# RWKV's threads: where five results are produced and used in the steps of the recurrence

## The chip, the cores and the metric

One core of one Trainium2 chip runs the program. The metric is device microseconds of one execution, the median of the runs shown.

## The reference

One layer of a bidirectional encoder over 256 positions of width 2048: a projection feeds three mixers (a gated MLP, a Hyena long convolution, RWKV-7), whose outputs are gated and merged, followed by a SwiGLU. The change lies in the RWKV mixer, whose recurrence is

```python
def step(s, inp):
    r_t, w_t, k_t, v_t, a_t, b_t = inp
    sa = jnp.einsum('dbhij,dbhj->dbhi', s, a_t)
    s = s * w_t[..., None, :] + sa[..., :, None] * b_t[..., None, :] + v_t[..., :, None] * k_t[..., None, :]
    return s, jnp.einsum('dbhij,dbhj->dbhi', s, r_t)

_, y = lax.scan(step, s0, (r, w, k, v, a, b))
```

It runs in both directions over 16 heads of 64 channels, and is followed by a norm per head, a bonus term `sum(r * k * r_k) * v` and a gate.

## The kernel before

All dense products are split into float32r parts: a weight piece of 4 k-tiles (128x512) is loaded by a DMA from SP, cast to `wh` on ScalarE (ACT, L222), and the rest `wl` is taken on VectorE (DVE) or GpSimd (POOL, L226). `dense` (L239 to L241) then issues three matmuls 128x256 per k-tile, and yields after each k-tile. The program of GpSimd, VectorE and ScalarE besides holds the recurrence's own work.

The recurrence is in chunks of 64 positions and treats two heads at a time; such a pair is called head 0 to 7 here (`j` in the code). It is written as five generators, each of which walks through all eight heads: `wkv_prep` (decays, keys, bonus), `wkv_scores` (score matmuls L667, their masked evictions L676, transposes of `bk`), `wkv_inverse` (a triangular inverse: 15 steps of two small VectorE operations, L733 and L736, called the substitution here, a round trip of the blocks through DRAM, L742 and L747, a VectorE transpose of what came back, L750, then matmuls L755 and L763), `wkv_chain` (L802, L813, then the four chunk steps: matmuls L855, L861, L874 with the VectorE results `T` L857, `UV` L865 and `sb` L879 between them) and `wkv_norm`. `threads` runs them in rounds: in each round every generator advances by one `yield 1`, and about four k-tiles (`ROUND = 4.0`, 12 matmuls) of the queued dense work are issued among them, so that TensorE has something to do while the other engines work.

```python
                with self.tc.issue_after(self.last.ins):
                    step = next(g, self)
```

So what a generator issues in a step can't stand ahead of the last dense matmul before that step on TensorE. It can stand behind it: each engine runs its instructions in a fixed order, but a scheduler makes that order when the program is built, from its own costs, and lets later instructions pass one whose inputs it takes to be late. The order of an engine is therefore read from the built program, not from the code. Dense work that the recurrence doesn't use up is issued behind it (`drain`).

PSUM tiles: `ps_dn` for the dense work, `ps_big` with two buffers for most of the rest, `ps_inv` and `ps_ch` for inverse and chain.

Of the kernel before, what the change touches and what calls it, by code (L numbers as in the profile page):

```python
# [12 lines left out]
AF = mybir.ActivationFunctionType  # L13
# [3 lines left out]
P = 128  # L17
T = 256
# [172 lines left out]
class Build:  # L191
# [359 lines left out]
    def wkv_prep(self, R, j, front, res):  # L551

        nc = self.nc
        rp = R["rp"]
        V, S, G = nc.vector, nc.scalar, nc.gpsimd
        tl = lambda sh, name, bufs=1: rp.tile([P] + sh, F32, tag=name, name=name, bufs=bufs)
        mult, add = ALU.mult, ALU.add
        rk2, v = front
        r, k = rk2[:, 0, :], rk2[:, 1, :]
# [9 lines left out]
        for i in range(2):  # L569
            for d in range(2):  # L570
                rows = slice(64 * d, 64 * d + 64)
                nc.tensor.matmul(pd[d][:, i * T:(i + 1) * T], wa[rows, i, :],
                                 R["lo"][rows, 1 + i, :], start=True, stop=True, tile_position=(64 * d, 0))
        for d in range(2):
            ps = pd[d]
            tw = tl([T], "tw")
            for i, z in enumerate((tw, ta[:, d, :])):
                c = 16 * i + 8 * d + j
                S.activation(z, ps[:, i * T:(i + 1) * T], AF.Tanh, bias=R["hb"][:, c:c + 1], scale=0.5)
            V.tensor_scalar(tw, tw, 0.5, 0.5, mult, add)  # L580
            if d == 0:
                V.tensor_tensor_scan(cum[:, 0, :], sm[:, :T], tw, 0.0, mult, add)
            else:
                V.tensor_tensor_scan(cum[:, 1, ::-1], sm[:, T:0:-1], tw[:, ::-1], 0.0, mult, add)
            yield 1

        sq = tl([T], "sq")
        S.activation(sq, k, AF.Square, scale=self.vec("k_k", j))
        ps = self.pst("big")
        nc.tensor.matmul(ps[:, :T], self.cst("bones"), sq, start=True, stop=True)  # L590
        yield 1
# [45 lines left out]
        rk = tl([T], "rk")  # L637
        G.tensor_tensor(rk, kd[:, 0, :], kd[:, 1, :], add)
        V.scalar_tensor_tensor(rk, r, self.vec("r_k", j), rk, mult, mult)
        ps = self.pst("big")  # L640
        nc.tensor.matmul(ps[:, :T], self.cst("bones"), rk, start=True, stop=True)
        bon = tl([T], "bon", 2)
# [67 lines left out]
    def wkv_inverse(self, R, j, st):  # L710


        nc = self.nc
        rp = R["rp"]
        V, S, D = nc.vector, nc.scalar, nc.sync
        tl = lambda sh, name, bufs=1: rp.tile([P] + sh, F32, tag=name, name=name, bufs=bufs)
        mult, add = ALU.mult, ALU.add
        d1, Mo = st[1:3]
        Z = tl([2, 2, P], "Z")
        N = Z[:, 1].rearrange("p a (b c) -> p (a b) c", c=16)  # L720
        yield 1
        src = d1.rearrange("d u (q s) e -> (d u q) s e", s=32)
        for i in range(4):
            b = 16 * (i % 2)
            D.dma_start(N[32 * i:32 * i + 32], src[:, b:b + 16, b:b + 16])
        Y, Yt = tl([8, 16], "Y"), Z[:, 0, 0, :40]
        D.dma_start(Y, self.t["rows"])
        yield 1
        yield 1
        for k in range(15):  # L730
            n, w = 15 - k, k // 2 + 1
            z = Yt[:, :w * n].rearrange("p (c t) -> p c t", t=n)
            first = V.tensor_tensor(z, N[:, k, k + 1:].unsqueeze(1).broadcast_to([P, w, n]), Y[:, :w, k:k + 1].broadcast_to([P, w, n]), mult)  # L733
            if k == 0:
                self.tc.keep_in_program_order(first)
            V.tensor_tensor(Y[:, :w, k + 1:], Y[:, :w, k + 1:], z, add)  # L736
            if k % 4 == 3:
                yield 1
        d2 = R["d2"][j % 2]
        for i in range(4):  # L740
            r, b = i // 2, i % 2
            D.dma_start(d2[:, b, :, r, 16 * b:16 * b + 16], Y[32 * i:32 * i + 32])  # L742
        yield 1
        yield from self.after("whole", j - 1)

        XX = tl([4, P], "XX")
        D.dma_start(Z[:, 0].rearrange("p d (u e) -> p (d u) e", e=32), d2.rearrange("(u q) b c r e -> (q b c r) u e", q=4))  # L747
        yield 1
        yield 1
        self.tc.keep_in_program_order(V.transpose(Z[:, 1].rearrange("p a b -> p (a b)"), Z[:, 0].rearrange("p a b -> p (a b)")))  # L750
        blocks = [(d, u, q) for d in range(2) for u in range(4) for q in range(4)]
        ps = self.pst("inv")
        for d, u, q in blocks:
            r, o = slice(32 * q, 32 * q + 32), slice(32 * u, 32 * u + 32)
            nc.tensor.matmul(ps[r, P * d + 32 * u:P * d + 32 * u + 32], Mo[r, d, o], Z[r, 1, d, o], start=True, stop=True,  # L755
                             tile_position=(32 * q, 32 * q))
        T0 = tl([2, P], "T0")
        S.copy(T0, ps[:, :2 * P].rearrange("p (d n) -> p d n", d=2))
        yield 1
        ps = self.pst("inv")  # L760
        for d, u, q in blocks:
            r, o = slice(32 * q, 32 * q + 32), slice(32 * u, 32 * u + 32)
            nc.tensor.matmul(ps[r, P * d + 32 * u:P * d + 32 * u + 32], T0[r, d, o], Z[r, 0, d, o], start=True, stop=True,  # L763
                             tile_position=(32 * q, 32 * q))
        V.tensor_tensor(XX[:, :2], Z[:, 0], ps[:, :2 * P].rearrange("p (d n) -> p d n", d=2), add)
        V.transpose(XX[:, 2:].rearrange("p a b -> p (a b)"), XX[:, :2].rearrange("p a b -> p (a b)"))
        st += XX,
        yield 1
        self.passed.add(("inverse", j))

    def wkv_chain(self, R, j, pre, st):

        nc = self.nc
        rp = R["rp"]
        V, S, G = nc.vector, nc.scalar, nc.gpsimd
        tl = lambda sh, name, bufs=1: rp.tile([P] + sh, F32, tag=name, name=name, bufs=bufs)
        mult, add = ALU.mult, ALU.add
        ident = self.cst("ident")
        v, wcs, bk, ar = pre[:4]
# [2 lines left out]
        at = lambda z, c, h: XX[:, z, 32 * (2 * h + c // 2):32 * (2 * h + c // 2) + 32]  # L782
        X, XT = lambda d, c, h: at(2 - d, c, h), lambda d, c, h: at(3 * d, c, h)
        XF = R["xf"]

        def place(q, d, b):

# [8 lines left out]
        ps = self.pst("inv")  # L796
        for (d, c, h) in units:
            hb = 1 - c % 2
            src, dst = (0, 1) if d == 0 else (1, 0)
# [7 lines left out]
        ps = self.pst("inv")  # L807
        for (d, c, h) in units:
            hb = 1 - c % 2
            src, dst = (0, 1) if d == 0 else (1, 0)  # L810
# [7 lines left out]
                (S.copy if d else V.tensor_copy)(place(q, d, 1 - d), u4(ps[32 * q:32 * q + 32, :P]))  # L818
        yield 1
        self.passed.add(("whole", j))  # L820

        UV = tl([2, 2, 2, P], "UV")
        ps = self.pst("big")
        for i in range(2):
            nc.tensor.transpose(ps[:, i * P:(i + 1) * P], v[:, i * P:(i + 1) * P], ident)
        for par in range(2):
            rows = slice(64 * par, 64 * par + 64)
            src = ps[rows, :T].rearrange("p (c n) -> p c n", n=P).unsqueeze(1).broadcast_to([64, 2, 2, P])
            (S.copy if par else V.tensor_copy)(UV[rows, :, :, par, :], src)

        self.passed.add(("v", j))

        at_step = lambda i: [(d, i if d == 0 else 3 - i) for d in range(2)]


# [14 lines left out]
        for i in range(NC_):  # L850
# [11 lines left out]
            for d, c in at_step(i):  # L862
                hb = 1 - c % 2
                rows = slice(64 * hb, 64 * hb + 64)
# [21 lines left out]
        ps = self.pst("big")  # L886
# [15 lines left out]
    def wkv_norm(self, R, j, pre, ych, ycl):  # L902
# [8 lines left out]
        nc.tensor.matmul(ps[:, :T], self.cst("bones"), yy, start=True, stop=True)  # L911
        V.tensor_tensor(yy, yy, ps[:, :T], ALU.subtract)
        sq2 = tl([T], "sq2")
        yield 1
        S.activation(sq2, yy, AF.Square)
        ps = self.pst("big")
        nc.tensor.matmul(ps[:, :T], self.cst("bones"), sq2, start=True, stop=True)
        pg = self.pst("big")
# [555 lines left out]
```

## Time and profile before

| | |
|---|---|
| runs | 2003.42, 2006.95, 2007.06 us; median 2006.95 us |
| profiled execution | 2000.44 us, its span 1998.7 us |
| busy in the span | TensorE 1892.7, VectorE 1387.7, ScalarE 1068.5, GpSimd 546.5 us |
| recurrence | about 440 to 1030 us of the span |

In the rows below, PE is TensorE's matmuls and PEld its weight loads; in windows, the first number is the length in us, and behind the engines come PEclk, DMA share and GB/s; a bracket at a row's end gives the engine's idle time just before it and what ended that. PEclk is the granted TensorE clock as a share of full speed.

### The profile page before, as it was taken

The numbers are of one execution on the slowest core, as the hardware profiler recorded it, in microseconds if no ns is written. First come the engines' busy times: TensorE is split into PE (matmuls) and PEld (weight loads), VectorE is DVE, ScalarE is ACT, GpSimd is POOL, SyncE is SP. The second block draws the span as 40 slices with busy tenths as digits, with TensorE's granted clock in tenths as the row PEclk, the third lists the DMA queues.
The fourth block names the chain that finished last, engine by engine and source line by source line (L and its number), as shares of the span: only waits on it lengthen the run. The fifth ranks groups of instructions, "written<-read, shape, count | busy, mean of one in ns | idle before, by whom it ended". The sixth has DMA issues, their size and how long they took to land.

```text
span 1998.7 us, 37486 instructions
## 1 busy us (share of the span) xinstructions
PE 1892.7 (95%) x13476; PEld 1679.0 (84%) x13476; DVE 1387.7 (69%) x2556; ACT 1068.5 (53%) x2142; POOL 546.5 (27%) x573
## 2 busy tenths in 40 slices
PE   8999999999879898989999999999999999999997
PEld 6788888879868787888898888888888888888886
DVE  7978798786775767566567777766666666655555
ACT  7665566555444454544445555555555555545443
POOL 3322322235645455545421121111111111100001
PEclk9999999999999899998999999999999999999999
DMA  8454454445433333333355565555555555666664
GB/s 262 158 169 153 135 157 152 138 140 186 123 103 111 90 104 88 115 97 95 97 164 190 190 229 188 188 190 190 191 190 190 190 191 190 189 185 186 188 185 136
DMA packets 215828, 320.39 MB, mean 160 GB/s; under 512 B 62198, under 2 KB 65784, under 8 KB 215640
## 3 DMA queue, kind: packets, MB, share of 16 engines
q1 hardware_dynamic: 209264, 306.13, 49.5%
q0 software_dynamic: 2032, 6.18, 1.0%
q10 hardware_dynamic: 4344, 5.67, 0.9%
q8 instruction: 106, 1.74, 0.4%
q14 instruction: 82, 0.67, 0.1%
HBM read 313.96 MB, written 3.93 MB: 159 GB/s over the span
## 4 chain that ended last, share of the span: by engine, by line
PE 49%; DMA 1%; DVE 1%; ACT 0%; issue 0%; DVEq 0%; POOL 0%; ACTq 0%; POOLq 0%
PE ps_dn L259 23%; PE ps_dn L260 12%; PE ps_big L259 8%; PE ps_big L260 4%; DMA w<-in_wo_dram 0%; PE ps_dn L239 0%; PE ps_dn L240 0%; PE ps_dn L241 0%; PE ps_dn L257 0%; PE ps_dn L256 0%; DVE x L1454 0%; DMA x<-in_xT_dram 0%; DVE wl L226 0%; DVEq L1469 0%; PE ps_ch L855 0%
## 5 line engine op out<-in xcount | busy, mean ns | idle before, releaser
L222 ACT CAST wh<-w 128x512 fp32r<-128x512 f32 x1148 | 704.6, 619 | 570.6 <-PE ps_dn L259 258.0
L226 DVE TENSOR_TENSOR wl<-w,wh 128x512 fp32r<-128x512 f32 x945 | 718.2, 768 | 380.6 <-ACT wh L222 371.8
L226 POOL TENSOR_TENSOR wl<-w,wh 128x512 fp32r<-128x512 f32 x203 | 271.1, 1340 | 378.7 <-ACT wh L222 335.7
L259 PE MATMUL ps_dn<-gw,wh 128*128 128x512 f32 x704 | 246.3, 392 | 0.0
L259 PE MATMUL ps_big<-gw,wh 128*128 128x512 f32 x704 | 246.0, 391 | 0.0
L270 PE MATMUL ps_dn<-hw,wh 128*128 128x512 f32 x640 | 232.1, 402 | 11.9 <-DVE x L400 7.0
L259 PE MATMUL ps_dn<-hid,wh 128*128 128x512 f32 x660 | 233.2, 396 | 0.0
L239 PE MATMUL ps_dn<-hw,wh 128*128 128x256 f32 x688 | 213.6, 311 | 0.0
L241 PE MATMUL ps_dn<-hw,wl 128*128 128x256 f32 x688 | 199.5, 290 | 3.3 <-DVE wl L226 2.6
L260 PE MATMUL ps_dn<-hid,wl 128*128 128x256 f32 x704 | 198.7, 282 | 0.0
L240 PE MATMUL ps_dn<-hw,wh 128*128 128x256 f32 x688 | 198.5, 289 | 0.0
L260 PE MATMUL ps_dn<-gw,wl 128*128 128x256 f32 x704 | 197.6, 281 | 0.0
L260 PE MATMUL ps_big<-gw,wl 128*128 128x256 f32 x704 | 197.4, 280 | 0.0
L271 PE MATMUL ps_dn<-hw,wl 128*128 128x256 f32 x640 | 180.0, 281 | 0.0
L259 PEld LDWEIGHTS ps_big<-gw,wh 128*128 128x128 f32 x704 | 131.8, 187 | 28.7
L259 PEld LDWEIGHTS ps_dn<-gw,wh 128*128 128x128 f32 x704 | 131.8, 187 | 28.6
L270 PEld LDWEIGHTS ps_dn<-hw,wh 128*128 128x128 f32 x640 | 121.2, 189 | 39.6 <-ACT th L1344 5.6
L259 PEld LDWEIGHTS ps_dn<-hid,wh 128*128 128x128 f32 x660 | 124.1, 188 | 30.0
L239 PEld LDWEIGHTS ps_dn<-hw,wh 128*128 128x128 f32 x688 | 134.4, 195 | 6.7 <-issue 3.1
L241 PEld LDWEIGHTS ps_dn<-hw,wl 128*128 128x128 f32 x688 | 134.4, 195 | 4.7 <-DVE wl L226 3.0
L240 PEld LDWEIGHTS ps_dn<-hw,wh 128*128 128x128 f32 x688 | 134.6, 196 | 1.1
L260 PEld LDWEIGHTS ps_dn<-gw,wl 128*128 128x128 f32 x704 | 133.4, 190 | 0.1
(404 smaller groups left out, 3714.9 us busy)
## 6 DMA issues: line engine op xcount, KB each, us to landing
w<-in_wgu_dram SPq DMA_DIRECT2D x352, 256.0 KB, 3.0
w<-in_wgt_dram SPq DMA_DIRECT2D x192, 256.0 KB, 3.0
w<-in_wdn_dram SPq DMA_DIRECT2D x176, 256.0 KB, 2.9
w<-in_wc_dram SPq DMA_DIRECT2D x108, 256.0 KB, 3.0
w<-in_wb_dram SPq DMA_DIRECT2D x96, 256.0 KB, 3.0
w<-in_wbr_dram SPq DMA_DIRECT2D x96, 256.0 KB, 2.7
w<-in_wo_dram SPq DMA_DIRECT2D x64, 256.0 KB, 3.1
w<-in_wav_dram SPq DMA_DIRECT2D x32, 256.0 KB, 3.6
```

Of the source, the lines that this page charges most:

```text
L222: nc.scalar.copy(wh[:, :m], w[:, :m])
L226: e.tensor_tensor(wl[:, :m], w[:, :m], wh[:, :m].bitcast(F32), ALU.subtract)
L239: mm(ps, wh[:, i, :], xh[:, k, :], start=(k == 0), stop=False)
L240: mm(ps, wh[:, i, :], xl[:, k, :], start=False, stop=False)
L241: self.last = mm(ps, wl[:, i, :], xh[:, k, :], start=False, stop=(k == nk - 1))
L259: mm(ps, wh[:, i, :], xk.rearrange("p a t -> p (a t)"), start=(k == 0), stop=False)
L260: mm(ps[:, :T], wl[:, i, :], xk[:, 0, :], start=False, stop=(k == nk - 1))
L270: mm(ps, wh[:, i, :], x[:, k].rearrange("p a t -> p (a t)"), start=(k == 0), stop=False)
L271: mm(ps[:, :T], wl[:, i, :], x[:, k, 0, :], start=False, stop=(k == nk - 1))
```

## The change

Five places in the threads. In `wkv_prep` the square `sq` is issued one step earlier, ahead of the yield, so that its matmul L590 comes a step after it; and a yield is put between `rk` (L639) and its matmul L641. In `wkv_inverse` a yield is put between the transpose L750 and the matmuls L755. In `wkv_chain` the two transposes of `v` (L825) and the copies into `UV` (L829) go from behind the second yield to the generator's start. In `wkv_norm` the square `sq2` (L915) goes ahead of a yield, and its matmul L917 stays behind it. No operation is added or removed. The rounds become 158 instead of 154.

```diff
@@ -582,10 +582,10 @@
                 V.tensor_tensor_scan(cum[:, 0, :], sm[:, :T], tw, 0.0, mult, add)
             else:
                 V.tensor_tensor_scan(cum[:, 1, ::-1], sm[:, T:0:-1], tw[:, ::-1], 0.0, mult, add)
-            yield 1
-
-        sq = tl([T], "sq")
-        S.activation(sq, k, AF.Square, scale=self.vec("k_k", j))
+
+                sq = tl([T], "sq")
+                S.activation(sq, k, AF.Square, scale=self.vec("k_k", j))
+            yield 1
         ps = self.pst("big")
         nc.tensor.matmul(ps[:, :T], self.cst("bones"), sq, start=True, stop=True)
         yield 1
@@ -637,6 +637,7 @@
         rk = tl([T], "rk")
         G.tensor_tensor(rk, kd[:, 0, :], kd[:, 1, :], add)
         V.scalar_tensor_tensor(rk, r, self.vec("r_k", j), rk, mult, mult)
+        yield 1
         ps = self.pst("big")
         nc.tensor.matmul(ps[:, :T], self.cst("bones"), rk, start=True, stop=True)
         bon = tl([T], "bon", 2)
@@ -748,6 +749,7 @@
         yield 1
         yield 1
         self.tc.keep_in_program_order(V.transpose(Z[:, 1].rearrange("p a b -> p (a b)"), Z[:, 0].rearrange("p a b -> p (a b)")))
+        yield 1
         blocks = [(d, u, q) for d in range(2) for u in range(4) for q in range(4)]
         ps = self.pst("inv")
         for d, u, q in blocks:
@@ -782,6 +784,17 @@
         at = lambda z, c, h: XX[:, z, 32 * (2 * h + c // 2):32 * (2 * h + c // 2) + 32]
         X, XT = lambda d, c, h: at(2 - d, c, h), lambda d, c, h: at(3 * d, c, h)
         XF = R["xf"]
+
+        UV = tl([2, 2, 2, P], "UV")
+        ps = self.pst("big")
+        for i in range(2):
+            nc.tensor.transpose(ps[:, i * P:(i + 1) * P], v[:, i * P:(i + 1) * P], ident)
+        for par in range(2):
+            rows = slice(64 * par, 64 * par + 64)
+            src = ps[rows, :T].rearrange("p (c n) -> p c n", n=P).unsqueeze(1).broadcast_to([64, 2, 2, P])
+            (S.copy if par else V.tensor_copy)(UV[rows, :, :, par, :], src)
+
+        self.passed.add(("v", j))
 
         def place(q, d, b):
 
@@ -818,18 +831,6 @@
                 (S.copy if d else V.tensor_copy)(place(q, d, 1 - d), u4(ps[32 * q:32 * q + 32, :P]))
         yield 1
         self.passed.add(("whole", j))
-
-        UV = tl([2, 2, 2, P], "UV")
-        ps = self.pst("big")
-        for i in range(2):
-            nc.tensor.transpose(ps[:, i * P:(i + 1) * P], v[:, i * P:(i + 1) * P], ident)
-        for par in range(2):
-            rows = slice(64 * par, 64 * par + 64)
-            src = ps[rows, :T].rearrange("p (c n) -> p c n", n=P).unsqueeze(1).broadcast_to([64, 2, 2, P])
-            (S.copy if par else V.tensor_copy)(UV[rows, :, :, par, :], src)
-
-        self.passed.add(("v", j))
-
         at_step = lambda i: [(d, i if d == 0 else 3 - i) for d in range(2)]
 
 
@@ -911,8 +912,8 @@
         nc.tensor.matmul(ps[:, :T], self.cst("bones"), yy, start=True, stop=True)
         V.tensor_tensor(yy, yy, ps[:, :T], ALU.subtract)
         sq2 = tl([T], "sq2")
-        yield 1
         S.activation(sq2, yy, AF.Square)
+        yield 1
         ps = self.pst("big")
         nc.tensor.matmul(ps[:, :T], self.cst("bones"), sq2, start=True, stop=True)
         pg = self.pst("big")
```

The orders of the engines move with it. TensorE around L755 of head 3, before: `L894` is the end of head 2's outputs, `L861` belongs to its chain; 12 of the 16 L894 stand 16 dense matmuls further ahead, of which the last two are shown.

```order
L241 MATMUL ps_dn<-hw,wl 128x256
L239 MATMUL ps_dn<-hw,wh 128x256
L755 MATMUL ps_inv<-Z,Mo 32x32 x32
L861 MATMUL ps_inv<-T_8933,xf 128x64 x2
L240 MATMUL ps_dn<-hw,wh 128x256
L241 MATMUL ps_dn<-hw,wl 128x256
L763 MATMUL ps_inv<-Z,T_8981 32x32 x32
L894 MATMUL ps_big<-sc,UV 64x64 x4
```

And in the changed program, where L755 is L757, L763 is L765, L894 is L895:

```order
L895 MATMUL ps_big<-sc,UV 64x64 x12
L239 MATMUL ps_dn<-hw,wh 128x256
L240 MATMUL ps_dn<-hw,wh 128x256
L241 MATMUL ps_dn<-hw,wl 128x256
L757 MATMUL ps_inv<-Z,Mo 32x32 x32
L862 MATMUL ps_inv<-T_8934,xf 128x64 x2
L239 MATMUL ps_dn<-hw,wh 128x256
L240 MATMUL ps_dn<-hw,wh 128x256
L765 MATMUL ps_inv<-Z,T_8981 32x32 x32
L895 MATMUL ps_big<-sc,UV 64x64 x4
```

The inverse's matmuls stand 3 dense matmuls behind the outputs instead of 16. The read that they need (`Z` from DRAM, L747 on SP) moved as well, from between the 371st and the 372nd load of a weight piece to one place earlier.

TensorE from v's transposes L825 to the first matmuls that read `UV`, L842, head 4, before:

```order
L241 MATMUL ps_dn<-hw,wl 128x256
L825 MATMUL ps_big<-consts,v 128x128 x2
L239 MATMUL ps_dn<-hw,wh 128x256
L240 MATMUL ps_dn<-hw,wh 128x256
L241 MATMUL ps_dn<-hw,wl 128x256
L239 MATMUL ps_dn<-hw,wh 128x256
L240 MATMUL ps_dn<-hw,wh 128x256
L241 MATMUL ps_dn<-hw,wl 128x256
L704 MATMUL ps_big<-consts,bk 128x128 x2
L842 MATMUL ps_ch<-UV,sc 64x64
L704 MATMUL ps_big<-consts,bk 128x128 x2
```

In the changed program the transposes (now L791) stand at the head's start, beside L802 (now L815):

```order
L240 MATMUL ps_dn<-hw,wh 128x256
L241 MATMUL ps_dn<-hw,wl 128x256
L791 MATMUL ps_big<-consts,v 128x128 x2
L815 MATMUL ps_inv<-XX,sc 32x32 x16
L239 MATMUL ps_dn<-hw,wh 128x256
```

and 18 dense matmuls, L813 and more follow before L842 (now L843):

```order
L241 MATMUL ps_dn<-hw,wl 128x256
L642 MATMUL ps_big<-rk,consts 128x256
L239 MATMUL ps_dn<-hw,wh 128x256
L240 MATMUL ps_dn<-hw,wh 128x256
L241 MATMUL ps_dn<-hw,wl 128x256
L843 MATMUL ps_ch<-UV,sc 64x64 x16
```

Between transposes and reader lay 6 dense matmuls; now 30 and other work lie there, and the 16 readers stand together.

VectorE in the chain of head 2 where head 3's substitution (L733, L736) begins, before, from the last VectorE `wl` ahead of it; `L627` and `L593` are preparation of head 4, `sb` and `T` are chain results for which TensorE waits:

```order
L226 TENSOR_TENSOR wl<-w,wh 128x512
L879 SCALAR_TENSOR_TENSOR sb_5765<-ps_inv,wc,consts 128x128
L627 SCALAR_TENSOR_TENSOR ta<-ta,cum 128x256
L593 TENSOR_SCALAR sq<-ps_big 128x256
L627 SCALAR_TENSOR_TENSOR ta<-ta,cum 128x256
L857 TENSOR_TENSOR T_8745<-ps_ch,KV 128x128
L733 TENSOR_TENSOR Z<-Z,Y 128x15
L328 TENSOR_SCALAR kk<-sq 128x256
L736 TENSOR_TENSOR Y<-Y,Z 128x15
```

and in the changed program, from right behind the same `sb` (L733 is L734, L736 is L737, L857 is L858):

```order
L734 TENSOR_TENSOR Z<-Z,Y 128x15
L226 TENSOR_TENSOR wl<-w,wh 128x512
L737 TENSOR_TENSOR Y<-Y,Z 128x15
L734 TENSOR_TENSOR Z<-Z,Y 128x14
L737 TENSOR_TENSOR Y<-Y,Z 128x14
L593 TENSOR_SCALAR sq<-ps_big 128x256
L734 TENSOR_TENSOR Z<-Z,Y 128x26
L328 TENSOR_SCALAR kk<-sq 128x256
L737 TENSOR_TENSOR Y<-Y,Z 128x2x13
L627 SCALAR_TENSOR_TENSOR ta<-ta,cum 128x256
L734 TENSOR_TENSOR Z<-Z,Y 128x24
L858 TENSOR_TENSOR T_8753<-ps_ch,KV 128x128
```

The substitution begins ahead of `T` instead of behind it, and the preparation stands between its operations. Over all eight heads 114 other operations stand inside the substitutions instead of 90.

## Rows read from the trace of the kernel before

**Rows 1.** Windows in and behind the recurrence: busy time (instructions) of PE, PEld, DVE, ACT, POOL

```profile
440.00:1030.00 590.00, 525.89 (x5594) 484.58 (x5593) 389.24 (x849) 278.41 (x620) 298.49 (x314) 0.95 0.39 112
1030.00:1998.00 968.00, 954.89 (x5516) 839.15 (x5514) 631.87 (x1035) 515.90 (x967) 111.83 (x143) 1.00 0.60 188
```

**Rows 2.** What TensorE waited for, 440 to 1030 us: total us, times, longest

```profile
PE ps_ch L855 <- DVE sb L879: 15.8, 10, 2.6
PE ps_inv L874 <- DVE UV L865: 6.7, 7, 2.0
PE ps_inv L755 <- DVE Z L750: 6.0, 4, 2.7
PE ps_big L667 <- DVE bon L643: 5.7, 1, 5.7
PE ps_inv L755 <- issue: 5.6, 3, 3.1
PE ps_big L641 <- DVE rk L639: 4.9, 2, 3.8
PE ps_big L917 <- ACT sq L915: 3.9, 2, 2.1
...
PE ps_ch L842 <- DVE UV L829: 2.7, 4, 0.9
```

**Rows 3.** A window of 8 us of dense matmuls

```profile
704.00:712.00 8.00, 8.00 (x67) 7.49 (x66) 2.21 (x5) 4.27 (x9) 5.15 (x4) 1.00 0.62 157
```

**Rows 4.** VectorE's copies of v into UV, line L829: count, ns min/median/max

```profile
L829 DVE COPY UV<-ps_big x8: 669/674/682, 581.7 to 983.1; 64x512 f32<-64x512 f32 x8
```

**Rows 5.** The read of Z from DRAM, line L747: who waits, landing time

```profile
DVE Z L750: 15.6, 6
...
DMA to landing us min/median/max: 2.5/3.5/4.7
```

**Rows 6.** Timeline, the transpose of Z and its matmuls in head 3; the matmuls in head 6

```profile
741.58 0.45 DVE L750 STREAM_TRANSPOSE Z<-Z 128x256 f32<-128x256 f32 x1 [1.55 <-DMA Z<-d]
742.12 0.74 PE L755 MATMUL ps_inv<-Z,Mo 32*32 32x32 f32 x64 [1.30 <-issue]
...
928.13 0.75 PE L755 MATMUL ps_inv<-Z,Mo 32*32 32x32 f32 x64 [0.42 <-DVE Z L750]
```

**Rows 7.** Timeline, head 0: the scores, and GpSimd's part of their input

```profile
524.80 1.16 PE L667 MATMUL ps_big<-ar,bk 64*128 64x128 f32 x16
521.47 1.76 POOL L630 TENSOR_TENSOR ar<-kk,E 128x256 f32<-128x256 f32 x2
```

**Rows 8.** Timeline, head 1: scores held by a PSUM buffer, VectorE and GpSimd then

```profile
557.06 2.07 PE L667 MATMUL ps_big<-ar,bk 64*128 64x128 f32 x14 [5.73 <-DVE bon L643]
553.55 3.12 DVE L736 TENSOR_TENSOR Y<-Y,Z 128x14 f32<-128x14 f32 x1
557.13 0.18 DVE L736 TENSOR_TENSOR Y<-Y,Z 128x26 f32<-128x26 f32 x1
559.94 0.68 DVE L676 TENSOR_TENSOR sc<-ps_big,wconsts 128x512 f32<-128x512 f32 x1
554.15 2.48 POOL L226 TENSOR_TENSOR wl<-w,wh 128x512 fp32r<-128x512 f32 x2
```

**Rows 9.** Timeline, head 3's norm: the square and its matmul

```profile
796.81 0.42 ACT L915 ACTIVATE sq<-y 128x256 f32<-128x256 f32 x1 [3.66 <-DVE y L912]
797.28 0.70 PE L917 MATMUL ps_big<-sq,consts 128*128 128x256 f32 x2 [2.14 <-ACT sq L915]
```

**Rows 10.** Timeline of VectorE, head 2's chain: preparation ahead of T

```profile
715.08 0.57 DVE L627 SCALAR_TENSOR_TENSOR ta<-ta,cum 128x256 f32<-128x256 f32 x1
715.56 0.41 DVE L593 TENSOR_SCALAR sq<-ps_big 128x256 f32<-128x256 f32 x1
```

**Rows 11.** Windows of 8 us: a full VectorE, then a stretch behind two waits

```profile
720.00:728.00 8.00, 4.82 (x29) 4.32 (x29) 7.93 (x27) 2.50 (x6) 4.16 (x4) 0.89 0.32 103
...
688.00:696.00 8.00, 8.00 (x127) 6.76 (x129) 4.20 (x8) 4.47 (x13) 1.99 (x2) 0.53 0.11 35
```

More of the change, by code (lines that the diff above doesn't have):

```diff
@@ L913, in wkv_norm @@
         sq2 = tl([T], "sq2")
+        S.activation(sq2, yy, AF.Square)
         yield 1
-        S.activation(sq2, yy, AF.Square)
         ps = self.pst("big")
```

## The prediction

> **What bounds the kernel now.** I read three views in turn. The windows first: behind the recurrence TensorE idles 13 us in 968, inside it 64 us in 590 at a mean granted clock of 0.95 [rows 1]. So the change works where there is something to gain, and since dense work is still left when the threads end, time there is TensorE's busy time plus its idle time: four more rounds only bring dense matmuls forward from the tail. Second, the waits of TensorE in that stretch [rows 2]. Those that the change names are L755 (6.0 + 5.6 us; the "issue" ones turn out to be the same wait), L641 (4.9), L917 (3.9) and L842 (2.7): 23.1 us. L590, whose square is also moved, is not among the waits. The larger part, 15.8 + 6.7 us on `sb` and `UV` in the chain, is left as it is. Third, the timeline around each named wait, beside the order of the two programs. That decides, for the kernel's scheduler has already put a matmul behind dense ones until it takes the input to be ready. What stalls are inputs later than it reckons. A yield written in the code helps only where it pushes the matmul past the place that the scheduler would give it anyway.
>
> **What a step covers.** 67 matmuls, nearly all dense, run in 8 us at full clock [rows 3]: 0.12 us apart, so the 12 of a round cover 1.44 us.
>
> **`sq` and `sq2`: 0.** With these two edits alone TensorE's order is the same row for row: L590 and L917 stand where they stood, and L911 to L917 keep their 18 dense matmuls. For L917 the trace says what was late: the square waited 3.66 us for VectorE's subtraction, which stood behind the substitution, and L917 idled 2.14 us [rows 9]. Nothing in the change brings that subtraction forward. Bounds: 0 and, should the shifted orders happen to spare both waits, -3.9 us.
>
> **v's transposes: -2.7.** Two transposes and two copies, VectorE's of 674 ns [rows 4], stood 6 to 12 dense matmuls ahead of L842, 0.7 to 1.4 us of cover against copies that run one after the other. In the changed order 30 to 69 dense matmuls lie between, 3.6 us or more, so the four waits go: -2.7 [rows 2]. The copies now stand at the chain's start on VectorE and ScalarE, beside the copies of the inverse; between L802 and L813, which waits for ScalarE there, the order has 18 to 57 dense matmuls, where 6 to 30 were. I price this side at 0; if a copy stood in L813's way in each head it would be 8 x 0.67 = +5.4.
>
> **The inverse's yield: -1.7.** L755 waits for the VectorE transpose, and that for a read of `Z` from DRAM: VectorE sits idle for it, 15.6 us in six heads, and the read takes 2.5 to 4.7 us to land [rows 5]. In head 3 the transpose began 1.55 us late and L755 1.30 us late right behind it [rows 6]. The yield stands behind the transpose, so the read isn't issued earlier in its thread. If L755 were pushed back a whole round everywhere, up to 1.44 us would go in each of the seven waits, 8.5 us in all, since three of them are longer than that and head 6's is 0.42 us [rows 6]. But in heads 0, 1, 3 and 5 the changed order gives L755 a place by readiness again: in head 3 it even stands 13 dense matmuls earlier behind head 2's outputs, as the read moved up by one weight piece too. Only in heads 4, 6 and 7 is the written step what holds it; counted from the start it stands there 6, 10 and 4 dense matmuls later, 0.7, 1.2 and 0.5 us, of which head 6 could use only the 0.4 it waited. That gives 0.7 + 0.4 + 0.5 and 0.1 for one matmul in head 2: -1.7. Bounds 0 and -8.5.
>
> **The bonus matmul, head 0: -1.6.** L641 idled 3.8 us for `rk` [rows 2]. In the changed order the score matmuls L667 come at the same dense place, ahead of L641. They need `ar`, whose second half GpSimd finished at 521.47 + 1.76 = 523.2 us, and began at 524.80 [rows 7]. So the wait moves from L641 to L667, and what is won is 524.8 - 523.2.
>
> **The bonus matmul, head 1: 0.** Before, scores waited 5.73 us for a `ps_big` buffer that held the bonus, because the eviction (L643) stood behind small VectorE operations, one of 14 elements that took 3.12 us while GpSimd ran two `wl` of 2.48 us; its like takes 0.18 [rows 8]. In the changed order scores go first and need no such buffer, but the next user, now L641, needs the one that the scores fill, and its eviction L676 stands behind 24 operations of the substitution, four more than in front of its place at 559.94. Four at 0.18 more, VectorE gets there at 560.7 us and has evicted at 561.3. TensorE would arrive at 553: the scores come up at 557.06 - 5.73 = 551.3, take 1.16 us [rows 7], and six dense matmuls follow. That is 8 us of waiting for 5.7 + 1.1. I take 0, since head 0's gain feeds in; bounds -6.9 and +1.4.
>
> **Crowding in the substitution: 0, up to +10.7.** 24 more operations stand among the substitutions of the changed order, mostly L627 and L593 of 0.57 and 0.41 us [rows 10]; at 0.45 us each, an estimate from these two rows, that is 10.7 us in the six heads where VectorE is full already (7.93 of 8 us, TensorE at 4.82 [rows 11]). What stands inside now stood just ahead of it before, in the same busy stretch, and as many chain results lie inside the substitutions as before (26). So I take 0 and keep +10.7 as a bound.
>
> Sum: -2.7 - 1.7 - 1.6 = -6.0 us. Against the profiled execution that is 2000.4 - 6.0 = 1994.4 us; that execution is 6.5 us quicker than the median of the runs, so against the median 2006.95 I predict **2001.0 us**, 0.3% faster. About 0.2% (4 us) is what a measurement of this kernel tells from no change.
>
> **The rivals.** *Full effect* (8 in 100): the yields cover what they are written for, and all 23.1 us of named waits go; 2006.95 - 23.1 = 1984 us. With the waits the clock would come back: behind head 2's wait at L755 the granted clock was 0.53 for 8 us, nearly all of it at the lower level of 1.2 GHz, so 3.8 us lost [rows 11]. For it: L755 waits for a read to land, which VectorE's queue doesn't lengthen. Against: L917 and half of the L755 keep the place that they had beside their neighbours in TensorE's order.
>
> *The waits stay* (31 in 100): order follows readiness, v's 2.7 us are won and lost again in a changed collision somewhere among the 22 us of chain waits; 2003 to 2011, say 2006 us. For it: those waits are single accidents of 1 to 2.6 us, and each head's collisions are dealt anew.
>
> *Slower* (23 in 100): the crowding decides. Place: the chain's L855, L861 and L874 while the next head's substitution runs. Each result queues on VectorE behind up to 1.8 us more (10.7 over six heads), and TensorE has one round of 1.44 us to cover it, which it uses up today. If TensorE feels the whole of it, 2006.95 - 6.0 + 10.7 = 2011.7 us; slower by over 0.2% it becomes once 10 of the 10.7 are felt, or fewer where the clock falls behind the longer waits as it did in [rows 11]. The Trainium skill's page "SBUF — State Buffer", section "Who interferes with whom", says that a VectorE operation with two SBUF inputs and a GpSimd one that reads SBUF exclude each other for a whole instruction. The 3.12 us of [rows 8] agree with it. It speaks against the change: an operation more among those of the substitution is one more chance to be held for a `wl` of GpSimd, which no step's cover would hide.
>
> **How the numbers follow.** The forecast has 38 in 100; its own range is 1997 to 2003, from v's term alone to L755's upper half. With the full effect, faster is 46 in 100; same 31, slower 23. The range, 1990 to 2014, takes in the rivals but for the full effect and the end of the slower one, 15 to 20 in 100.
>
> **What would show it.** Right: no wait at L842; L755 still among the largest with 8 to 11 us; L917 unchanged in kind; at head 0 a wait of some 4 us at L667 in place of L641. In head 1 a wait at L641 for L676 in place of L667's for L643. Wrong: L755's waits gone (the place in the order then matters less than I say), or chain waits on `sb` and `UV` that together move by more than 6 us from today's 22.5; TensorE's idle time between 440 and 1030 us is the sum to watch, 64 now, 58 expected.

## The result and the profile after

The changed kernel took **2017.56 us** (median of 7 runs, 2011.85 to 2029.83) against 2006.95 for the kernel before (7 runs, 2002.27 to 2016.15): ratio 1.0059, 95% interval 1.0042 to 1.0075. It is slower by 10.6 us; forecast were 2001.0 us and faster. A ratio here is not the quotient of the two medians; the two can differ by some 0.1%.

The profiled execution of the changed kernel took 2020.21 us, its span is 2018.3 us, 19.6 longer than that of the kernel before. The medians are only 10.6 us apart: the trace of the kernel before (2000.44 us) is of an execution that was quicker than any of its seven runs, so what follows, read from this pair of traces, is larger than the median loss. Its lines are shifted: L641 is L642, L667 is L668, L755 is L757, L842 is L843, L855, L861 and L874 are L856, L862 and L875, L917 is L918. First the window of the recurrence, as in [rows 1].

```profile
440.00:1030.00 590.00, 517.14 (x5481) 479.65 (x5480) 378.78 (x825) 269.59 (x604) 292.42 (x309) 0.92 0.36 108
```

TensorE idles 72.9 us in the recurrence (590 less 517.14) where it was 64.1: 8.8 more, and the granted clock is 0.92 for 0.95. Behind the recurrence it idles 13.9 us for 13.1. Over the whole span TensorE is busy 1903.5 us for 1892.7: so about half of the 19.6 us is idle time, and the other half (10.8) busy time, for the same matmuls at a lower clock. What TensorE waited for, as in [rows 2] (total us, times, longest):

```profile
PE ps_ch L856 <- DVE sb L880: 15.7, 8, 3.8
PE ps_inv L757 <- DVE Z L751: 10.4, 4, 3.6
PE ps_inv L862 <- DVE T L858: 7.8, 4, 2.2
PE ps_big L642 <- DVE sc L677: 5.8, 2, 5.3
...
PE ps_big L668 <- DVE Z L734: 5.2, 1, 5.2
...
PE ps_inv L875 <- DVE UV L866: 3.3, 2, 2.8
PE ps_inv L757 <- issue: 3.1, 3, 1.3
...
PE ps_big L668 <- POOL ar L630: 2.1, 1, 2.1
```

L843 (L842 before) is gone from the list, as the change meant. Everything else that it names is there, and larger: L757 13.5 us for 11.6, L918 5.3 for 3.9, and in the front, where heads 0 and 1 are prepared, L642 and L668 with some 14 us for 10.9. In the chain, waits for `T` have grown to 7.8 us, from 3.2 in the kernel before,

```profile
PE ps_inv L861 <- DVE T L857: 3.2, 4, 1.6
```

and those for `UV` have fallen from 6.7 to 3.3. The largest pair of waits stands in one stretch. These are windows of 8 us in the front, of the kernel before:

```profile
552.00:560.00 8.00, 2.94 (x18) 2.72 (x19) 7.45 (x20) 0.07 (x1) 4.63 (x7) 0.72 0.47 150
560.00:568.00 8.00, 8.00 (x66) 7.66 (x65) 6.51 (x21) 4.29 (x10) 3.36 (x4) 0.85 0.20 45
```

And of the changed kernel:

```profile
552.00:560.00 8.00, 3.66 (x22) 3.17 (x22) 7.90 (x13) 0.00 (x0) 6.65 (x9) 0.57 0.27 91
560.00:568.00 8.00, 3.60 (x15) 3.19 (x17) 5.42 (x25) 0.62 (x1) 1.17 (x1) 0.50 0.19 61
```

Before, one wait of 5.73 us [rows 8] took most of the first window, and from 560 us on TensorE ran 66 matmuls in a window. After, it ran 15 there, at the lower level of 1.2 GHz throughout (0.50). The rows of that place in the changed kernel, VectorE, GpSimd and TensorE:

```profile
550.49 1.05 DVE L595 SCALAR_TENSOR_TENSOR kk<-rk,kks,kk 128x256 f32<-128x256 f32 x1
...
551.94 3.00 DVE L737 TENSOR_TENSOR Y<-Y,Z 128x15 f32<-128x15 f32 x1
...
555.27 0.41 DVE L628 SCALAR_TENSOR_TENSOR bk<-ta,kk 128x256 f32<-128x256 f32 x1
...
552.36 1.32 POOL L630 TENSOR_TENSOR ar<-kk,E 128x256 f32<-128x256 f32 x2
553.63 1.26 POOL L226 TENSOR_TENSOR wl<-w,wh 128x512 fp32r<-128x512 f32 x1
...
555.41 2.08 PE L668 MATMUL ps_big<-ar,bk 64*128 64x128 f32 x16 [5.22 <-DVE Z L734]
...
564.40 1.22 PE L642 MATMUL ps_big<-rk,consts 128*128 128x256 f32 x2 [5.33 <-DVE sc L677]
```

Head 1's scores L668 need `ar` and `bk`, and both are made from `kk`. VectorE has the second half of `bk` only at 555.68 (555.27 + 0.41), the first 0.41 us sooner. Two things make it late. In front of it an operation of the substitution, of 15 elements, takes 3.00 us while GpSimd runs `ar` and `wl`. And `kk` itself comes at 551.54 (550.49 + 1.05). In the kernel before `kk` was done at 547.16, 4.4 us sooner, and the same `bk` at 550.38, ahead of the substitution:

```profile
546.68 0.48 DVE L595 SCALAR_TENSOR_TENSOR kk<-rk,kks,kk 128x256 f32<-128x256 f32 x1
...
548.60 1.78 DVE L628 SCALAR_TENSOR_TENSOR bk<-ta,kk 128x256 f32<-128x256 f32 x2
```

So the scores wait 5.22 us, from 550.19 us on. The late `kk` is the larger part of it: `ar` was there only at 553.68 (552.36 + 1.32), so without the hold they would still have waited some 3 us (an estimate from these rows). The bonus matmul L642, now behind them, waits 5.33 us more for their eviction L677, which stands behind the substitution; that was held three times more, for 0.75, 1.19 and 1.19 us, between 556.7 and 559.9 us, while GpSimd ran L1352 and two `wl`. The two waits have little between them. In windows of 1 us the clock falls inside the first one, at 553.1 us, and is back only at 570.2; in the kernel before it was down from 555.5 to 562.3 us.

The front is not the whole of it. Up to 620 us TensorE idles 30.5 us for 25.5 in this pair of traces, and from there to 1030 us 42.4 for 38.6.

### The profile page after: what moved, and what is told of

Read it like the earlier page. It is cut to its first block, busy times and chain, and to the rows that moved or that the text cites. A ratio compares the mean times of both kernels' runs of the same rounds, so it can differ in the third digit from the quotient of the medians.

```text
span 2018.3 us, 37484 instructions
## 1 busy us (share of the span) xinstructions
PE 1903.5 (94%) x13476; PEld 1690.8 (84%) x13476; DVE 1392.2 (69%) x2556; ACT 1069.2 (53%) x2142; POOL 545.7 (27%) x573
## 5 line engine op out<-in xcount | busy, mean ns | idle before, releaser
L226 DVE TENSOR_TENSOR wl<-w,wh 128x512 fp32r<-128x512 f32 x945 | 722.2, 772 | 384.0 <-ACT wh L222 377.6
L226 POOL TENSOR_TENSOR wl<-w,wh 128x512 fp32r<-128x512 f32 x203 | 271.0, 1339 | 391.2 <-ACT wh L222 345.2
L259 PE MATMUL ps_dn<-gw,wh 128*128 128x512 f32 x704 | 246.3, 391 | 0.0
L259 PE MATMUL ps_big<-gw,wh 128*128 128x512 f32 x704 | 246.0, 391 | 0.0
L259 PE MATMUL ps_dn<-hid,wh 128*128 128x512 f32 x660 | 233.2, 396 | 0.0
L239 PE MATMUL ps_dn<-hw,wh 128*128 128x256 f32 x688 | 217.3, 316 | 1.0 <-DVE rk L400 1.0
L240 PE MATMUL ps_dn<-hw,wh 128*128 128x256 f32 x688 | 201.3, 293 | 0.0
L259 PEld LDWEIGHTS ps_dn<-gw,wh 128*128 128x128 f32 x704 | 131.7, 187 | 28.9
L259 PEld LDWEIGHTS ps_big<-gw,wh 128*128 128x128 f32 x704 | 131.6, 187 | 28.9
L270 PEld LDWEIGHTS ps_dn<-hw,wh 128*128 128x128 f32 x640 | 121.1, 189 | 39.4 <-ACT th L1345 5.6
L259 PEld LDWEIGHTS ps_dn<-hid,wh 128*128 128x128 f32 x660 | 124.0, 188 | 30.1
L239 PEld LDWEIGHTS ps_dn<-hw,wh 128*128 128x128 f32 x688 | 137.5, 200 | 8.4 <-issue 4.8
L240 PEld LDWEIGHTS ps_dn<-hw,wh 128*128 128x128 f32 x688 | 137.7, 200 | 1.4 <-issue 0.4
```

The costliest lines, as they stand in the source:

```text
L226: e.tensor_tensor(wl[:, :m], w[:, :m], wh[:, :m].bitcast(F32), ALU.subtract)
L239: mm(ps, wh[:, i, :], xh[:, k, :], start=(k == 0), stop=False)
L240: mm(ps, wh[:, i, :], xl[:, k, :], start=False, stop=False)
L259: mm(ps, wh[:, i, :], xk.rearrange("p a t -> p (a t)"), start=(k == 0), stop=False)
L270: mm(ps, wh[:, i, :], x[:, k].rearrange("p a t -> p (a t)"), start=(k == 0), stop=False)
```

## The experiments

All runs compute the whole of the reference. Ratios are to the kernel before on the same chip.

**One edit at a time.** The bonus yield alone, the inverse's yield alone, v's move alone (the fourth and fifth piece of the diff above), the two squares alone (the first and the last):

```diff
# only_rk
         V.scalar_tensor_tensor(rk, r, self.vec("r_k", j), rk, mult, mult)
+        yield 1
# only_z
         self.tc.keep_in_program_order(V.transpose(Z[:, 1]...
+        yield 1
```

> The kernel before with the bonus yield alone (a step between `rk` and its matmul). Theory F (the front): the yield lets the scores pass the bonus matmul, so head 0 waits at its scores for GpSimd's `ar`, and head 1 at its scores for `Z` and then at the bonus matmul for the scores' own eviction. In the changed kernel these front waits are 14 to 15 us against 11 before, so this edit alone should cost 4 to 8 us: 2011 to 2015 against 2007, ratio 1.002 to 1.004. Theory R (every order deals the collisions anew, no edit has a cost of its own): the front waits may look the same, but the whole lies anywhere within 8 us of the kernel before, and the loss of each edit alone doesn't add up to the whole's 10.6 us. Theory B (bounds of the prediction): the edit is worth -1.6 us, ratio 0.999.

> The kernel before with the inverse's yield alone (a step between the transpose of `Z` and the first matmul that uses it). Theory F (the loss is the front's): this edit doesn't touch the order of heads 0 and 1, so no loss, 2003 to 2008 us. Theory Z (the step moves the first matmul back by a round but its head's later steps too, so the next head's substitution falls on this head's chain): waits at L755 as long as before (11 to 14 us), chain waits longer, 2010 to 2014 us. Prediction: -1.7 us, ratio 0.999.

> The kernel before with v's transposes and copies at the chain's front alone. Prediction: L842's wait of 2.7 us goes, nothing else, ratio 0.9987. Theory V (the two copies stand in front of the chain's own copies on VectorE and ScalarE): up to 5.4 us slower, ratio 1.003, with longer waits at L802 and L813. Theory R (orders deal the collisions anew): L842's wait goes, and as much or more comes at other places, within 8 us of the kernel before.

> The kernel before with the two squares a step earlier alone; TensorE's order stays the same row for row. Prediction and theory F: 0, within 0.2% of the kernel before (2003 to 2011 us). Theory S (the squares take ScalarE from evictions that TensorE waits for): 4 us or more slower, with longer waits released by ScalarE.

Measured: the bonus yield 2021.58 us, ratio 1.0074 (1.0055 to 1.0093); the inverse's yield 2012.72, 1.0026 (1.001 to 1.0041); v's move 2013.11, 1.0033 (1.002 to 1.0046); the squares 2006.04, 1.0000 (0.9984 to 1.0015). The squares cost nothing. Each of the others loses by itself, the bonus yield some twice the 4 to 8 us of theory F, and the three together (14.9 + 5.2 + 6.6 us by these ratios) lose less than their sum: they do not add.

In the inverse's yield alone TensorE's waits changed so:

```profile
PE ps_inv L862 <- DVE T L858: 11.2, 6, 2.2
PE ps_inv L756 <- DVE Z L750: 8.6, 4, 2.7
...
PE ps_inv L756 <- issue: 2.9, 2, 1.9
```

L756, for which the step was written, waits 11.5 us where it waited 11.6: the step covers nothing. But `T` rose from 3.2 to 11.2 us. One of these waits, of 2.17 us, on VectorE and GpSimd:

```profile
714.91 0.17 DVE L736 TENSOR_TENSOR Y<-Y,Z 128x14 f32<-128x14 f32 x1
...
715.34 0.95 DVE L733 TENSOR_TENSOR Z<-Z,Y 128x26 f32<-128x26 f32 x1
...
716.41 0.70 DVE L736 TENSOR_TENSOR Y<-Y,Z 128x26 f32<-128x26 f32 x1
...
717.99 0.28 DVE L858 TENSOR_TENSOR T<-ps_ch,KV 128x128 f32<-128x128 f32 x1
...
714.91 1.34 POOL L226 TENSOR_TENSOR wl<-w,wh 128x512 fp32r<-128x512 f32 x1 [0.96 <-ACT wh L222]
716.21 1.83 POOL L629 TENSOR_TENSOR bk<-kd,cum 128x256 f32<-128x256 f32 x2
```

`T` stands behind the next head's substitution and its preparation, as foreseen; unforeseen is how long those take. Operations of 0.17 us become 0.70 and 0.95, each ending with an operation of GpSimd (`wl`, and the first of the two `bk`).

v's move alone shows where its 2.7 us went in head 0. The wait for `UV` at L842 is gone, and `KV`, the next result of the chain, is late in its place, by 2.4 us:

```profile
592.98 0.26 ACT L829 COPY xf<-ps_inv 32x128 f32<-32x128 f32 x1 [0.46 <-DVE xf L829]
...
593.90 0.59 ACT L846 COPY KV<-ps_ch 128x512 f32<-128x512 f32 x1
...
594.54 0.48 PE L861 MATMUL ps_inv<-KV,xf 128*128 128x64 f32 x1 [2.40 <-ACT KV L846]
```

ScalarE's copies of the inverse (`xf`) wait for VectorE's, and KV's copy stands behind them. In the kernel before those of `xf` were done at 580.98, ahead of L842, which began at 582.46 and had waited 0.71 us for v's copies.

**One edit left out.** The changed kernel without each of the three yields or moves:

```diff
# no_rk: the changed kernel, without its second piece
-        yield 1
# no_z: without its third piece
-        yield 1
# no_v: v's block back behind the chain's second yield
```

> The changed kernel without the bonus yield, all other edits in. Theory F (the loss is the front's, made by this yield): the front's waits are again 10 to 11 us, and the time is at most the kernel before's, 2000 to 2007 us, ratio 0.997 to 1.000. Theory R (every order deals the collisions anew): the front's waits go back too, but the total doesn't follow from it; anywhere within 2003 to 2018 us.

> The changed kernel without the inverse's yield. Theory F: the loss of the front stays, 2013 to 2018 us, ratio 1.003 to 1.005. Theory Z (this yield pushes a head's later steps onto the next head's): the loss goes, 2004 to 2008 us. Theory R: anywhere within 2003 to 2018 us, and what leaves L755's waits comes up in the chain's.

> The changed kernel without v's move. Prediction's term: slower than the changed kernel by the 2.7 us of the waits for `UV`, ratio 1.007. Theory V (the copies at the chain's front cost up to 5.4 us): faster than the changed kernel, 2010 to 2014 us. Theory R: anywhere within 2003 to 2018 us.

Measured: without the bonus yield 2012.79 us, 1.0035 (1.002 to 1.0051); without the inverse's yield 2021.44, 1.0072 (1.005 to 1.0093); without v's move 2028.36, 1.0104 (1.0077 to 1.0132). Only the bonus yield's absence helps, and less than theory F had it: 2012.79 lies above its 2000 to 2007 us, so the yield isn't the whole loss. The other two came out above all that was expected of them. The kernel without v's move has some 9 us of its loss in another place (last section).

**The front.** The bonus yield in heads 0 and 1 alone in the kernel before; in heads 2 to 7 alone in the changed kernel; and, in the kernel before, the two operations that make `rk` a step up in place of the matmul a step down:

```diff
# rk_front (rk_late: if j > 1)
+        if j < 2:
+            yield 1
# rk_up: in the loop over d, ahead of its last yield, and no longer behind it
+            if d:
+                rk = tl([T], "rk")
+                G.tensor_tensor(rk, kd[:, 0, :], kd[:, 1, :], add)
+                V.scalar_tensor_tensor(rk, r, self.vec("r_k", j), rk, mult, mult)
             yield 1
```

> The kernel before with the bonus yield in heads 0 and 1 alone. The yield alone in all heads cost 14.6 us; its timeline was 10.5 us behind at 570 us, that is, behind head 1's waits. Theory F (the scores that pass the bonus matmul in the two heads of the front, and the clock behind their waits): 9 to 14 us slower, 2016 to 2021 us, front waits of about 14 us. Theory R (orders deal collisions anew, all along): 3 to 7 us slower, the same as any other edit.

> The changed kernel with the bonus yield in heads 2 to 7 alone. Theory F: the front is back to the kernel before's, and with it 5 to 6 us of the loss go: 2011 to 2013 us, as the changed kernel without the yield (2012.8). Theory R: no such tie; 2005 to 2022 us. If the yield costs in the later heads instead, it stays at 2017 us.

> The kernel before with the two operations that make `rk` moved a step up in place of the matmul a step down; TensorE's order stays the same row for row. Theory F (it is the place in TensorE's order that costs, not the step): no loss, and what `rk` is ready earlier shortens the waits at L641 (4.9 us) and so the bonus eviction that head 1's scores wait for (5.7 us): 2000 to 2006 us. If GpSimd and VectorE, which are full there, only swap one late operation for another: within 0.2%, 2003 to 2011 us.

Measured: in two heads alone 2019.93 us, 1.0045 (1.0021 to 1.0069); in the other six alone 2013.21, 1.002 (0.9999 to 1.0041), where the whole change has 1.0059; `rk` a step up 2013.52, 1.0006 (0.9983 to 1.0029), against 2009.57 for the kernel before on this chip. So two of eight heads make 9 us by the first run and 7.8 us (0.0039 of 2007, by the intervals some 5 us either way) by the second; the whole yield, left out above, made 4.8 (0.0024). The 9 us is the weakest of these: that run's trace has 9.4 us more in a stage that no edit touches (last section). But the traces show the front directly. From 440 to 620 us, the kernel before, the yield in two heads, the yield in the other six:

```profile
440.00:620.00 180.00, 154.52 (x1503) 142.76 (x1502) 127.02 (x236) 85.70 (x182) 100.19 (x110) 0.95 0.45 135
440.00:620.00 180.00, 148.29 (x1303) 136.97 (x1301) 129.60 (x229) 78.32 (x163) 95.65 (x102) 0.90 0.43 128
440.00:620.00 180.00, 152.29 (x1368) 142.00 (x1366) 128.21 (x233) 82.41 (x171) 102.04 (x106) 0.93 0.45 135
```

TensorE idles 25.5, 31.7 and 27.7 us, at 0.95, 0.90 and 0.93 of the clock; in the changed kernel it is 30.5 at 0.90. The yield's loss is in the front. Moving `rk` up gained nothing, where theory F had 2000 to 2006 us; its wait is again 4.9 us, so it is late by its inputs and not by its step.

**A blind step.** One more step behind the chain's last result, where TensorE waits for nothing:

```diff
         S.copy(y2, ps[:, :T])
         yield 1
+        yield 1
```

> A blind: the kernel before with one more step behind the chain's last result, where TensorE waits for nothing, so that the heads' steps fall otherwise against each other as in each of the edits. Theory R (orders deal the collisions anew, and the kernel before has a good deal): 3 to 9 us slower, as the inverse's yield alone (5.7) and v's move alone (6.1), from waits at other places. Theory Z (those two edits cost by what they move): within 0.2% of the kernel before, or the 1.4 us of a round.

Measured 2005.22 us against 2009.57, 0.998 (0.996 to 1.0). The waits were dealt anew (3.3 us at L802, where the kernel before has none), and the time didn't rise. This speaks against theory R, that any other order is slower; one order more doesn't refute it. That the edits cost by what they move fits all runs, but is argued.

**The buffer.** The bonus sums of heads 0 and 1 in a PSUM buffer of the chain, in the kernel before and in the changed kernel, and together with the blind step:

```diff
-        ps = self.pst("big")
+        ps = self.pst("ch" if j < 2 else "big")
         nc.tensor.matmul(ps[:, :T], self.cst("bones"), rk, start=True, stop=True)
```

> The kernel before with the bonus sums of heads 0 and 1 in a PSUM buffer of the chain, which is free then, so that head 1's scores don't wait for the bonus eviction; TensorE's order stays the same row for row. Theory B (what binds head 1 in the front is that one buffer): the 5.7 us at L667 go, and some 1 to 3 us of the lower clock behind them, 1998 to 2001 us against 2007, ratio 0.996 to 0.997. If another wait takes its place (scores' own eviction on VectorE, behind the held substitution): within 0.2%.

> The changed kernel with the bonus sums of heads 0 and 1 in a PSUM buffer of the chain; TensorE's order stays that of the changed kernel. Theory B: head 1's wait at the bonus matmul for the scores' eviction (5.3 us) goes, the wait of the scores for VectorE's `bk` (5.2 us) stays, the clock comes back 8 us sooner: 2008 to 2011 us, ratio 1.001 to 1.002 (changed kernel: 1.0059). If the wait only moves on to the next user of the score buffers: 2016 to 2018 us.

> Both things that did no harm or some good to the kernel before: a step more behind the chain's last result (ratio 0.998) and the bonus sums of heads 0 and 1 in the chain's PSUM buffer. If they add: 1995 to 2000 us, ratio 0.994 to 0.996. If the blind step was chance: as the buffer alone.

Measured: the kernel before 2004.95 us, 0.9994 (0.9974 to 1.0013); the changed kernel 2019.46, 1.006 (1.0034 to 1.0085); with the blind step 2007.96, 1.0012 (0.9993 to 1.003). In the kernel before theory B falls. The wait for the bonus eviction went, and in its place came a longer one:

```profile
PE ps_big L667 <- DVE sc L676: 8.1, 1, 8.1
```

Bonus sums and scores are both emptied by VectorE (L643, L676), whichever buffer holds them, and VectorE is late there. In the changed kernel a wait of 4.1 us at the next scores took the place of the 5.3 at L642. Its time settles less: its trace, and that of the run with the blind step, also have the 9.4 us of the last section.

**GpSimd's share.** During the threads GpSimd takes 0.6 of the weight splits (L226). Halved, in the changed kernel without the bonus yield, in the kernel before and in the changed kernel; and at 0.15 in the kernel before:

```diff
-        self.pool_share = 0.6
+        self.pool_share = 0.3
```

> The changed kernel without the bonus yield (1.0035), with GpSimd taking 0.3 in place of 0.6 of the weight splits during the threads. Theory H (the chain's `T` and `sb` are late because VectorE is held for as long as GpSimd splits): waits for `T` and `sb` fall from 21 to under 14 us, 2004 to 2009 us. Theory L (VectorE is late by its own load): some 47 more splits of 0.7 us stand on VectorE, the waits rise above 25 us, over 2018 us.

> The kernel before with GpSimd taking 0.3 in place of 0.6 of the weight splits during the threads. Theory H (GpSimd's splits hold VectorE, and VectorE's late results are what TensorE waits for): 1983 to 1995 us, ratio 0.988 to 0.994; the chain's waits, 27.6 us at share 0.6, fall to some 20. If the gain of the changed kernel without the bonus yield (1.0035 to 0.989) belongs to that order alone: 2003 to 2011 us.

> The changed kernel with GpSimd's share at 0.3. Theory H: its loss of 10.6 us was a loss by late VectorE results, so against the kernel before at the same share it is at most 4 us slower, 1983 to 1997 us. Theory F (the scores ahead of the bonus matmul cost by themselves): some 8 us stay, 1993 to 2003 us.

> The kernel before with GpSimd's share at 0.15. If holding is all of it: a further 4 to 10 us under share 0.3. If VectorE's own load sets the limit from here (it takes some 25 more splits of 0.7 us): 2 to 15 us above share 0.3.

Measured: the changed kernel without the bonus yield **1985.35 us**, 0.989 (0.9869 to 0.9912); the kernel before 1994.74, 0.9931 (0.991 to 0.9953); the changed kernel 1988.18, 0.9903 (0.9881 to 0.9924); the kernel before at 0.15 1986.9, 0.990 (0.988 to 0.992). In all three orders the time fell as theory H has it, in the first below its range, and the change's loss is gone with it: from 10.6 us slower it is 6.6 us faster than the kernel before at the same share. The two intervals overlap, so a gain of the change there is likely, not shown; that it no longer loses 0.6% is shown. What the share does is seen in GpSimd's splits, VectorE's splits and the substitution (busy us, mean ns), in the kernel before, 440 to 1030 us, at 0.6:

```profile
L226 POOL TENSOR_TENSOR wl<-w,wh 128x512 fp32r<-128x512 f32 x158 | 206.8, 1315 | 175.3 <-ACT wh L222 154.2 <-PE ps_inv L813 8.7 <-ACT T L758 4.9
L226 DVE TENSOR_TENSOR wl<-w,wh 128x512 fp32r<-128x512 f32 x67 | 61.4, 966 | 46.6 <-ACT wh L222 41.2 <-DMA w<-in_wbr_dram 3.2 <-DMA Z<-d 1.9
L736 DVE TENSOR_TENSOR Y<-Y,Z 128x30 f32<-128x30 f32 (+10 forms) x120 | 45.7, 380 | 2.1
L733 DVE TENSOR_TENSOR Z<-Z,Y 128x30 f32<-128x30 f32 (+10 forms) x120 | 41.1, 342 | 2.5 <-issue 0.3
```

at 0.15:

```profile
L226 POOL TENSOR_TENSOR wl<-w,wh 128x512 fp32r<-128x512 f32 x52 | 69.8, 1346 | 106.3 <-ACT wh L222 102.2 <-PE ps_inv L874 2.7 <-issue 1.2
...
L226 DVE TENSOR_TENSOR wl<-w,wh 128x512 fp32r<-128x512 f32 x183 | 144.2, 807 | 75.8 <-ACT wh L222 71.1 <-DMA Z<-d 3.3 <-PE ps_dn L240 0.3
L736 DVE TENSOR_TENSOR Y<-Y,Z 128x30 f32<-128x30 f32 (+10 forms) x120 | 35.5, 296 | 1.3
L733 DVE TENSOR_TENSOR Z<-Z,Y 128x30 f32<-128x30 f32 (+10 forms) x120 | 34.2, 285 | 1.3
```

VectorE has 116 more splits and is busy 83 us longer with them, but the same 240 operations of the substitution take 69.7 us in place of 86.8, and what TensorE waits for comes sooner. The share also empties GpSimd's queue, so that its own results could come sooner; VectorE's waits for them speak against that as the gain, for they don't shrink (6.2 us at 0.6, 7.2 at 0.15, in these 590 us). No run moves the splits without both. Waits at share 0.3, the kernel before:

```profile
PE ps_ch L855 <- DVE sb L879: 10.1, 10, 1.8
PE ps_inv L755 <- issue: 7.3, 4, 2.9
...
PE ps_inv L755 <- DVE Z L750: 4.5, 4, 2.5
...
PE ps_ch L842 <- DVE UV L829: 1.9, 4, 0.9
```

and the changed kernel:

```profile
PE ps_ch L856 <- DVE sb L880: 11.2, 8, 3.0
PE ps_big L642 <- DVE sc L677: 4.1, 1, 4.1
...
PE ps_big L668 <- DVE Z L734: 3.8, 1, 3.8
...
PE ps_big L668 <- DVE bk L628: 3.5, 1, 3.5
...
PE ps_inv L757 <- DVE Z L751: 3.1, 3, 1.2
...
PE ps_inv L757 <- issue: 1.3, 3, 0.6
```

Here L757 waits 4.4 us for 11.8, which is what the inverse's yield was written for (the other edits are in too), and L843 not at all for 1.9. The front's two waits are still there, but 3.8 and 4.1 us for 5.2 and 5.3, and one of 3.5 us for `bk` in head 0; the kernel before waits 9.9 us at these places at this share (6.6 at L641, 3.3 at L667).

## Why the prediction was wrong

The step that failed is **"the bonus matmul, head 1: 0"**, and with it "head 0: -1.6". Head 1's place was worked out on the old timeline: scores that come up at 551.3 us with `bk` there, then the bonus matmul at 553 us with 8 us of waiting. But the scores' inputs moved too. Head 1's preparation came 4.4 us later on VectorE, `bk` fell behind the start of the substitution and an operation that was held for 3.00 us, and the scores waited 5.22 us. Then L642 waited 5.33: the eviction, reckoned for 561.3 us, was done at 564.35, since the substitution was held again, and 25 of its operations ran ahead of it for 18 before, seven more and not four. Together that is 10.55 us, where the sum had 8 and the kernel before 6.86. In head 0 the wait did move to L668 for `ar`, as written, but at 2.1 us with 1.0 at L239 and 0.5 at L642 it is 3.6 us for 3.8 and not 1.6 less. The waits alone, 3.7 us more, broke the bound of +1.4; and the sum had no term for the clock, which was at 0.57 and 0.50 for 16 us of this place. Taken out of heads 0 and 1, the yield gives back 7.8 us, of idle time and clock together.

**v's transposes, -2.7.** No wait at L842: right. The copies' price at the chain's start, taken as 0 with a bound of +5.4, was wrong: alone the edit costs 6.6 us, of which the trace shows 2.4 at KV, 2.8 more for `T`, 1.5 more for `UV` and 2.1 more at L755, against 6.0 less at `sb`, L917 and L842.

**The inverse's yield, -1.7.** That the step would not serve L755, since the read isn't issued earlier, was right (11.5 us for 11.6 alone), and -1.7 was not seen. What failed is that the step was given no price: alone it costs 5.2 us, by 8.0 us more of waits for `T`, less some 5 us of those for `UV`.

**Crowding, 0 up to +10.7.** In the changed kernel the chain's waits for `sb` and `UV` together fell by 3.5 us, inside the 6 that I allowed, but `T`, which I hadn't put on that list, rose by 4.6. The rival *slower* named the right place and the right hold, and its 2011.7 us was nearer than the forecast; but by the runs without the yield (4.8 us) and without it in heads 0 and 1 (7.8) about half to three quarters of the 10.6 us lay elsewhere, in the front. The mis-sized quantity was the hold: I priced an operation among the substitution at 0.45 us, its time when not held.

**`sq` and `sq2`, 0.** Right: 1.0000, with TensorE's order unchanged.

**The clock.** In 590 us of recurrence it was 0.92 for 0.95. I had its price only in rivals, from [rows 11]; it made about half of the difference between the two spans (10.8 of 19.6 us).

The sentence of the Trainium skill, page "SBUF — State Buffer", section "Who interferes with whom", that a VectorE operation with two SBUF inputs and a GpSimd one that reads SBUF exclude each other for a whole instruction, is borne out by more than the 3.12 us of [rows 8]: with a third of GpSimd's splits the substitution's mean fell from 362 to 290 ns (86.8 and 69.7 us over 240). It should have weighed more: with half of GpSimd's share the change no longer loses.

Not settled: how much of the share's gain is the shorter holds and how much what else moves with the splits; why the three edits together cost less than apart, and how the loss of v's move and of the inverse's yield splits between holds and a crowded queue; the share was not halved for each of them alone.

## What to carry to other kernels

A step more between a producer and its matmul also moves every step behind it; before pricing the wait that it covers, ask what then passes in front (here the scores, whose own input was later still) and follow that input in the new order, not on the old timeline. Price a wait together with the clock behind it, above all two waits with little between. And where many waits end on one engine, look first at what makes that engine late: one number, GpSimd's share of the splits, was worth 12 to 29 us, where the best placing of steps tried here gained 0.2%, and turned the same five edits from a loss of 10.6 us into none.

## What the runs showed of the hardware that was not expected

The same matmuls run at two paces at the full granted clock. In a stage far behind the recurrence, L259 in the kernel before and in the kernel without v's move:

```profile
L259 PE MATMUL ps_big<-gw,wh 128*128 128x512 f32 x704 | 246.0, 391 | 0.0
...
L259 PE MATMUL ps_big<-gw,wh 128*128 128x512 f32 x704 | 250.7, 399 | 0.0
```

The granted clock is 1.00 in both. With the other buffer (`ps_dn`, 251.0 for 246.3) that is 9.4 us, and all six runs of that kernel were at 2022 us or above. No edit touches this stage. The slower pace stands in five of the twenty traces: besides this one, in the kernel before with the yield in two heads, with `rk` a step up, and with the chain's buffer and the blind step, and in the changed kernel with the chain's buffer. In three of these the traced execution was the slowest of its kernel's twelve runs (2025.69, 2017.78 and 2017.46 us), so the pace may change from one execution to the next; each kernel has one trace, and how many of its other runs hold the 9.4 us is not known. What sets the pace was not tried.
